# First two tile pairs of each feed-forward stage as plain products, with the sums of x formed beside them

## The chip, the cores and the metric

The kernel runs on one NeuronCore of a Trainium2 chip. The metric is device time in microseconds (us) of one execution, as the median of repeated runs. Times inside an execution come from one profiled execution, counted from the start of its span.

## The reference

One decoder layer for 512 tokens of width 1024, in float32:

```python
x = layer_norm(ALPHA * x + 0.5 * swiglu(x, ffn1_w_gate, ffn1_w_up, ffn1_w_down), ln1_g, ln1_b)
h = x @ w_in                     # q, f, i, g (512 each), conv_val, conv_gate (512 each)
mix = concat(hgrn2(q, f, i, g), conv_module(conv_val, conv_gate)) @ w_out
x = layer_norm(ALPHA * x + mix, ln2_g, ln2_b)
x = layer_norm(ALPHA * x + 0.5 * swiglu(x, ffn2_w_gate, ffn2_w_up, ffn2_w_down), ln3_g, ln3_b)
# swiglu(x) = (silu(x @ w_gate) * (x @ w_up)) @ w_down, hidden width 2816
```

The change lies in the two feed-forward stages (FFN1, FFN2), in their products with `w_gate` and `w_up`.

## The kernel before, in words

**Split operands.** Every float32 operand of a product is split into a high part (a cast on ScalarE, ACT, `cast` L65) and a low part (raw minus high, on VectorE, DVE, `rest` L68; some on POOL). A product of two operands is three matmuls: high x high, high x low, low x high. The splits of one 128x1024 weight tile are kept in a pool `parts` of six slots (`whi`, `wlo`); a slot is written again once TensorE (PE) has read it. The raw weights come through a pool `raws` of two buffers, loaded by SP's queue.

**Tile pairs and seven products.** The hidden width 2816 is 11 pairs of 128-column tiles. For pair `f`, the gate weights (`s` = 0) and the up weights (`s` = 1) are one `Quad` each: four blocks b11, b12, b21, b22, where the first figure is the half of the 1024 inputs and the second the tile of the pair. x is cut likewise into a11, a12, a21, a22 (first figure: half of the tokens, second: half of the inputs); class `Halves` holds these parts. A 2x2 block product is made from seven block products instead of eight (`SEVEN`, `product` L397): p1 = a11 b11, p2 = a12 b21, and five products of sums, as p7 = s3 t3, p5 = s1 t1. The sums of the weights t1 to t4 are formed and split by `Quad.inner`, those of x (s1 to s4) by `Halves.sums`, on DVE. One block product is 4 x 3 = 12 matmuls of 256 columns, so one tile pair (gate and up) is 2 x 7 x 12 = 168 matmuls. `Pair.steps` and `gate_up` combine the products in PSUM into silu(gate) x up.

**The first pair of each stage** is done in two parts: `early` issues p1 and p2 of gate and up (48 matmuls), which need no sums; `ffn` issues the rest (`LATER`), which needs s1 to s4. Pairs 1 to 10 run in the order `USUAL`.

**The start.** SP loads x in four quarters of 512 KB and the first two quads in pieces of 256 and 512 KB, in an order written out by hand (L544 on); then the residual rows `xres` (4 x 512 KB), then the weights of pair 1. POOL's queue loads `vecs` (72 KB). On DVE and ACT the few instructions that form `lb` from `vecs` (L579 to L586) stand ahead of the first splits.

**From one stage to the next.** `rows_out` ends a stage: the last four weight tiles of the down projection are kept, and each of the four token tiles is finished by turns (products, then `add` and `norm` on DVE and POOL). The finished token tile is transposed on PE (`transposed` L259, `transposed_halves` L273), and split into the next operand. PE's order there is written by hand: `follow` gives matmuls of the next stage, of which some are issued ahead of the transposes of the last two token tiles, by the estimates `NORM_WAITS`. At the end of FFN1 it is `four_halved` (the first four products of the mixing stage, in token halves); at the end of the mixing stage, ahead of FFN2, it is `begin`, which gives p1 and p2.

Of the kernel before, what the change touches and what calls it, by code (L numbers as in the profile page):

```python
# [23 lines left out]
NP = NF // 2  # L24
H = T // 2
# [16 lines left out]
BANKS1 = (((0, 2), (1, 3)), ((4, 6), (5, 7))), ((4, 5, 6, 7), (0, 1, 2, 3))  # L42
BANKS2 = (((2, 6), (3, 7)), ((0, 4), (1, 5))), ((0, 1, 4, 5), (2, 3, 6, 7))
# [7 lines left out]
def decoder_layer(ctx, tc, x_tok, x_q, vec, bcast, ng, w_gu1, w_d1, w_i, w_g, w_col, w_o, w_gu2, w_d2, out):  # L51
# [37 lines left out]
    class Quad:  # L89
# [16 lines left out]
        def outer(self, one_by_one=False):  # L106
            if not one_by_one:
                self.both(("b11", "b21"), self.raw[:, 0:4:3, :])
                return
            hi, lo = (t.rearrange("p (a b) -> p a b", a=2) for t in pair_of_parts())  # L110
            self.name(("b11", "b21"), hi, lo)

            def step(i):
                split(self.raw[:, 3 * i, :], hi[:, i, :], lo[:, i, :], nc.vector)
            return step
# [16 lines left out]
    def ahead(n):  # L132

        while todo and sum(r[0] for r in ready) < n:
            what, *args = todo.popleft()
            if what == "unit":
                ready.append([1, fetch(*args)])
            elif what == "quad":
                q = Quad(*args)
                q.load(0, 4)  # L140
                q.outer()
                q.inner()
                ready.append([3, q.of])
            elif what == "two":
                qs = [Quad(a) for a in args]
                for q in qs:
                    q.load(0, 4)
                for q in qs:
                    q.outer()
                    ready.append([1, q.of])  # L150
                todo.extendleft(("inner", q, r) for q, r in reversed(list(zip(qs, list(ready)[-2:]))))
            else:
                q, r = args
                q.inner()
                r[0] += 2
# [4 lines left out]
    def plan_quads(srcs):  # L160
        todo.extend(("quad", s) for s in srcs)

    def plan_two(srcs):
        todo.append(("two", *srcs))
# [9 lines left out]
    plan_quads([w_gu1[f, s] for f in range(1, NP) for s in range(2)])  # L174
# [8 lines left out]
    plan_two([w_gu2[0, s] for s in range(2)])  # L183
    plan_quads([w_gu2[f, s] for f in range(1, NP) for s in range(2)])
# [38 lines left out]
    class Halves:  # L223


        def __init__(self):
            a = [slot(f"xa{i}", (4, 4, H), F32R, f"a{'hl'[i]}") for i in range(2)]
            b = [slot(f"xb{i}", (3, 4, H), F32R, f"b{'hl'[i]}") for i in range(2)]
            self.raw = [slot(t, (2, 4, H), F32, "xr") for t in ("v", "c")]
# [741 lines left out]
```

## Time and profile before

| | us |
|---|---|
| median of 3 runs | 987.46 (987.25 to 988.12) |
| the profiled execution | 987.96 |
| its span | 986.1 |
| PE busy | 934.5 |
| DVE busy | 743.2 |
| ACT busy | 397.8 |

The profiled execution is 0.50 above the median, and 1.86 longer than its span. The page gives for each engine its busy time, and a line of 40 digits, each the busy share of one fortieth of the span (24.65 us) in tenths; PEclk is the granted TensorE clock in the same slices. Matmul records overlap (a matmul's record is longer than the time to the next start), so the rate of PE is read from the starts.

### The profile page before, as it was taken

The numbers are of one execution on the slowest core, as the hardware profiler recorded it, in microseconds if no ns is written. First come the engines' busy times: TensorE is split into PE (matmuls) and PEld (weight loads), VectorE is DVE, ScalarE is ACT, GpSimd is POOL, SyncE is SP. The second block draws the span as 40 slices with busy tenths as digits, with TensorE's granted clock in tenths as the row PEclk, the third lists the DMA queues.
The fourth block names the chain that finished last, engine by engine and source line by source line (L and its number), as shares of the span: only waits on it lengthen the run. The fifth ranks groups of instructions, "written<-read, shape, count | busy, mean of one in ns | idle before, by whom it ended". The sixth has DMA issues, their size and how long they took to land.

```text
span 986.1 us, 14697 instructions
## 1 busy us (share of the span) xinstructions
PE 934.5 (95%) x6096; PEld 855.0 (87%) x6096; DVE 743.2 (75%) x987; ACT 397.8 (40%) x577; POOL 120.4 (12%) x107
## 2 busy tenths in 40 slices
PE   3699999999999999999999999599999999999996
PEld 3599999999888888988888978499999999988885
DVE  5999888887834149799988668988888888762407
ACT  4465555554712113312231632555545555631200
POOL 9000000000000014531252103100000000000002
PEclk9699999999999999999999999799999999999999
DMA  7232323232443322321141050223223231443202
GB/s 258 86 127 91 126 87 128 86 105 89 139 150 86 106 65 86 108 76 53 25 128 40 26 189 1 86 86 112 103 87 128 87 129 65 129 150 102 90 22 85
DMA packets 21202, 96.69 MB, mean 98 GB/s; under 512 B 2368, under 2 KB 2368, under 8 KB 15760
## 3 DMA queue, kind: packets, MB, share of 16 engines
q1 hardware_dynamic: 21024, 95.43, 29.3%
q8 instruction: 47, 0.77, 0.3%
q0 software_dynamic: 112, 0.34, 0.1%
q14 instruction: 19, 0.16, 0.1%
HBM read 93.66 MB, written 2.10 MB: 97 GB/s over the span
## 4 chain that ended last, share of the span: by engine, by line
PE 74%; DVE 15%; issue 4%; POOL 2%; DMA 2%; ACT 2%; POOLq 0%; DVEq 0%; ACTq 0%
PE bank L397 44%; PE bank L190 9%; PE bank L189 9%; PE bank L188 9%; DVE bank L729 4%; PE bank L746 2%; DVE xres L335 2%; DVE wlo L68 1%; POOL wlo L68 1%; DMA raw<-w_col 1%; DMA vecs<-vec 1%; DVE bl L68 1%; DVE m L778 1%; POOL rstd L216 1%; DVE diag L786 1%
## 5 line engine op out<-in xcount | busy, mean ns | idle before, releaser
L68 DVE TENSOR_TENSOR wlo<-raw,whi 128x1024 fp32r<-128x1024 f32 (+1 forms) x144 | 174.0, 1213 | 146.4 <-ACT whi L65 146.2
L65 ACT CAST whi<-raw 128x1024 fp32r<-128x1024 f32 (+1 forms) x166 | 172.3, 1041 | 259.7 <-PE bank L190 140.7
L397 PE MATMUL bank<-bh,whi 128*128 128x256 f32 x528 | 152.0, 288 | 20.3 <-ACT bh L65 18.9
L397 PE MATMUL bank<-ah,whi 128*128 128x256 f32 x528 | 151.6, 287 | 9.8 <-ACT whi L65 9.5
L397 PE MATMUL bank<-bl,whi 128*128 128x256 f32 x528 | 151.9, 288 | 3.5 <-DVE bl L68 3.5
L397 PE MATMUL bank<-al,whi 128*128 128x256 f32 x528 | 151.3, 287 | 1.0 <-DVE al L278 0.8
L397 PE MATMUL bank<-bh,wlo 128*128 128x256 f32 x528 | 151.5, 287 | 0.8 <-DVE wlo L68 0.8
L397 PE MATMUL bank<-ah,wlo 128*128 128x256 f32 x528 | 151.2, 286 | 0.3 <-DVE wlo L68 0.3
L188 PE MATMUL bank<-whi,hp 128*128 128x512 f32 x320 | 124.7, 390 | 0.0
L190 PE MATMUL bank<-whi,hp 128*128 128x512 f32 x320 | 124.5, 389 | 0.0
L189 PE MATMUL bank<-wlo,hp 128*128 128x512 f32 x320 | 124.5, 389 | 0.0
L397 PEld LDWEIGHTS bank<-bh,whi 128*128 128x128 f32 x528 | 103.5, 196 | 21.0 <-ACT bh L65 19.3
L397 PEld LDWEIGHTS bank<-ah,whi 128*128 128x128 f32 x528 | 103.2, 195 | 10.1 <-ACT whi L65 9.5
L397 PEld LDWEIGHTS bank<-bl,whi 128*128 128x128 f32 x528 | 103.5, 196 | 4.1 <-DVE bl L68 4.1
L397 PEld LDWEIGHTS bank<-al,whi 128*128 128x128 f32 x528 | 103.1, 195 | 1.6 <-DVE al L278 1.1
L397 PEld LDWEIGHTS bank<-bh,wlo 128*128 128x128 f32 x528 | 103.5, 196 | 1.1 <-DVE wlo L68 1.1
L397 PEld LDWEIGHTS bank<-ah,wlo 128*128 128x128 f32 x528 | 103.0, 195 | 0.8 <-DVE wlo L68 0.8
L729 DVE SCALAR_TENSOR_TENSOR bank<-u,vecs,bank 128x512 f32<-128x512 f32 x120 | 82.1, 748 | 0.2
L68 DVE TENSOR_TENSOR wlo<-t,whi 128x1024 fp32r<-128x1024 f32 x44 | 54.6, 1242 | 24.9 <-ACT whi L65 24.9
L65 ACT CAST whi<-t 128x1024 fp32r<-128x1024 f32 x44 | 46.1, 1048 | 66.3 <-PE bank L397 62.7
L189 PEld LDWEIGHTS bank<-wlo,hp 128*128 128x128 f32 x320 | 60.1, 188 | 12.5
L188 PEld LDWEIGHTS bank<-whi,hp 128*128 128x128 f32 x320 | 60.1, 188 | 12.4
(184 smaller groups left out, 1772.6 us busy)
## 6 DMA issues: line engine op xcount, KB each, us to landing
raw<-w_gu SPq DMA_DIRECT2D x42, 1024.0 KB, 4.8
raw<-w_d SPq DMA_DIRECT2D x44, 512.0 KB, 3.6
raw<-w_col SPq DMA_DIRECT2D x16, 512.0 KB, 3.5
raw<-w_o SPq DMA_DIRECT2D x8, 512.0 KB, 3.6
xr<-x_q SPq DMA_DIRECT2D x4, 512.0 KB, 7.1
xres<-x_tok SPq DMA_DIRECT2D x4, 512.0 KB, 9.5
gb<-bcast SPq DMA_DIRECT2D x4, 512.0 KB, 4.9
raw<-w_i SPq DMA_DIRECT2D x4, 512.0 KB, 3.5
```

What stands on the lines that cost most here:

```text
L65: nc.scalar.copy(hi, raw)
L68: engine.tensor_tensor(lo, raw, hi.bitcast(F32), op=ALU.subtract)
L188: nc.tensor.matmul(ps, lhsT=lh, rhs=rh, start=first, stop=False)
L189: nc.tensor.matmul(ps, lhsT=lh, rhs=rl, start=False, stop=False)
L190: nc.tensor.matmul(ps, lhsT=ll, rhs=rh, start=False, stop=last)
L216: nc.gpsimd.tensor_tensor(r, r, negh.broadcast_to([P, n]) if n > 1 else negh, op=ALU.pow)
L335: nc.vector.scalar_tensor_tensor(xres[i][:, s], xres[i][:, s], r, bias[:, s], op0=ALU.mult, op1=ALU.add)
L397: nc.tensor.matmul(ps, lhsT=l[:, k, :], rhs=r[:, k, :], start=first and k == 0 and j == 0, stop=k == 3 and j == 2, skip_group_check=True)
L729: nc.vector.scalar_tensor_tensor(accs[n], us[n][:, j:j + T], vecs[:, w:w + 1], accs[n], op0=ALU.mult, op1=ALU.add)
L746: nc.tensor.matmul(ps[:, g, :], lhsT=k[:, h, sl], rhs=q[:, h, sl], start=True, stop=True)
L778: nc.vector.tensor_tensor(ov, ov, tv, op=ALU.mult)
L786: nc.vector.copy_predicated(diag[h], masks[:, n:n + 1, :].broadcast_to([P, NT, P]), ps)
```

## The change

1. Pairs 0 and 1 of each FFN (`PLAIN = 2`) are made as plain products: for each of the two tiles of gate and up, eight blocks of 128 inputs times all 512 tokens, three matmuls each, into one PSUM bank per tile (`plain`: 96 matmuls of 512 columns for a pair). `Halves` therefore keeps a21 too, in the place of s4; s4 is split later, in pair 2, by `last_sum`. `sums` forms the others while the plain pairs run.
2. In FFN1, pair 0's x and weights come in five steps of growing size (one, one, two, two, two of the eight input blocks); each step is one load of x and two of weights, and is split as it comes. PE takes the input blocks in order, over four banks at once.
3. In FFN2, pair 0 is what `begin` now gives: plain too, but in token halves (192 matmuls of 256 columns), the first half ahead of and between the transposes of the last two token tiles.
4. The weights' plan has entries `plain` (2 slots) and `seven` (3 slots) in place of `quad`, `two` and `inner`; banks and slots of both FFNs become the same.

```diff
+        def plain(self):
+            self.both(("b11", "b12"), self.raw[:, 0:2, :])
+            self.both(("b22", "b21"), self.raw[:, 2:4, :])
+        def pieces(self):
...
+            def load(half, a, b):
+                q, sl = slice(2 * half, 2 * half + 2), slice(a * P, b * P)
+                nc.sync.dma_start(out=self.raw[:, q, sl], in_=self.src[:, q, sl])
+            def step(half, a, b):
+                q, sl = slice(2 * half, 2 * half + 2), slice(a * P, b * P)
+                split(self.raw[:, q, sl], hi[half][:, :, sl], lo[half][:, :, sl], nc.vector)
...
+    def plan_quads(src, first):
+        todo.extend(("plain" if f < PLAIN else "seven", src[f, s]) for f in range(first, NP) for s in range(2))
...
+        def rows(self, k, kk=slice(None)):
+            return [t[:, 1:3, kk] if k else t[:, 0:4:3, kk] for t in self.parts]
...
-            self.part("s4", r12)
+        def last_sum(self):
+            self.part("s4", self.quarter(0, 1))
...
+    def plain(banks, x, ws):
+        for ps, (w, l) in zip(banks, ((w, l) for w in ws for l in range(2))):
+            for k in range(NK):
+                xh, xl = x.rows(k // 4, k % 4)
+                mm3(ps, *tile_parts(w, l, k), xh, xl, k == 0, k == NK - 1)
+                yield MM3
+    def begin(begun, x, banks):
+        ahead(4)
+        ws = [unit_now() for _ in range(2)]
+        begun.extend(bank(i, 2, H) for i in banks)
+        for t in range(2):
+            for ps, (w, l) in zip(begun, ((w, l) for w in ws for l in range(2))):
+                for k in range(NK):
+                    xh, xl = x.of[f"a{t + 1}{k // 4 + 1}"]
+                    mm3(ps[:, t], *tile_parts(w, l, k), xh[:, k % 4], xl[:, k % 4], k == 0, k == NK - 1)
+                    yield MM3 / 2
+        ahead(AHEAD)
...
             with tc.manual_schedule(engines={PE}):
-                ahead(3)
-                h.append(h_of(0))
-                for ns in LATER:
...
+                plain_gate_up(begun)
+                for f in range(1, PLAIN):
+                    ahead(4)
+                    ws = [unit_now() for _ in range(2)]
+                    ahead(3)
+                    got = [bank(i, 2, H) for i in chain(*zip(*PAIR_BANKS[f % 2]))]
+                    run(plain(got, x, ws))
+                    plain_gate_up(got)
...
+        for half, a, b in ((0, 0, 1), (0, 1, 2), (0, 2, 4), (1, 0, 2), (1, 2, 4)):
+            raw = x1.raw[half][:, a:b]
+            nc.sync.dma_start(out=raw, in_=x_q[half, :, a:b])
+            for load, _ in pieces:
+                load(half, a, b)
+            xh, xl = x1.rows(half, slice(a, b))
+            split(raw.rearrange("p k t c -> p t k c"), xh, xl, nc.vector)
+            for _, step in pieces:
+                step(half, a, b)
+        begun = [bank(i, 2, H) for i in range(4)]
+        for k in range(NK):
+            xh, xl = x1.rows(k // 4, k % 4)
+            for ps, (w, l) in zip(begun, ((w, l) for w in w0 for l in range(2))):
+                mm3(ps, *tile_parts(w, l, k), xh, xl, k == 0, k == NK - 1)
+        ahead(2)
+        x1.sums()
+        ahead(3)
```

**Three places in the engines' orders.** First, PE in FFN1's pair 0, where the kernel before turns from p2 to p7 (bank0 to bank3 are PSUM banks, `ah`, `al` parts of x, `bh`, `bl` parts of its sums, `whi_N`, `wlo_N` parts of weights). Before:

```order
L397 MATMUL bank1_173<-ah_83,whi_99 128x256
L397 MATMUL bank1_173<-al_84,whi_99 128x256
L397 MATMUL bank1_173<-ah_83,wlo_100 128x256
L397 MATMUL bank2_171<-bh_85,whi_127 128x256
L397 MATMUL bank2_171<-bl_86,whi_127 128x256
L397 MATMUL bank2_171<-bh_85,wlo_128 128x256
```

and at the 49th matmul of the change:

```order
L185 MATMUL bank3_153<-ah_83,whi_101 128x512
L186 MATMUL bank3_153<-al_84,whi_101 128x512
L187 MATMUL bank3_153<-ah_83,wlo_102 128x512
L185 MATMUL bank0_150<-ah_83,whi_99 128x512
L186 MATMUL bank0_150<-al_84,whi_99 128x512
L187 MATMUL bank0_150<-ah_83,wlo_100 128x512
```

Here PE went on with a sum of x (`bh_85`); now it goes on with the second half of the plain weights (`whi_99`), and no sum of x stands in PE's order until pair 2.

Second, DVE at the start of the change (`vecs` is the small load of POOL's queue, `xr` raw x, `raw` raw weights):

```order
L595 TENSOR_TENSOR mx_286<-vecs_79 128x4
L596 TENSOR_TENSOR e_287<-vecs_79,mx_286 128x4
L597 TENSOR_TENSOR e_287<-vecs_79,mx_286 128x4
L69 TENSOR_TENSOR al_84<-xr_87,ah_83 128x2x256
L69 TENSOR_TENSOR wlo_98<-raw_95,whi_97 128x2x128
L69 TENSOR_TENSOR wlo_102<-raw_96,whi_101 128x2x128
L599 TENSOR_TENSOR mx_286<-e_287 128x4
L600 RECIPROCAL mx_286<-mx_286 128x4
L601 TENSOR_TENSOR lb_80<-e_287,mx_286 128x4
L602 TENSOR_SCALAR oml_81<-lb_80 128x4
L69 TENSOR_TENSOR al_84<-xr_87,ah_83 128x2x256
```

All seven small instructions stood ahead of the first split; now three do, and four stand behind the first step. The step is of 512 and twice 256 elements a partition, where it was 1024 and twice 512.

Third, DVE ahead of FFN2, from the split of the second token tile to the norm of the last (`xres3`; `raw_5266` and `raw_5276` are the up weights of pair 0 and the gate weights of pair 1):

```order
L282 TENSOR_TENSOR al_5086<-bank7_5239,ah_5085 128x4x128
L69 TENSOR_TENSOR wlo_5269<-raw_5266,whi_5268 128x1024
L69 TENSOR_TENSOR wlo_5273<-raw_5266,whi_5272 128x1024
L69 TENSOR_TENSOR wlo_5279<-raw_5276,whi_5278 128x1024
L69 TENSOR_TENSOR wlo_5283<-raw_5276,whi_5282 128x1024
L324 SCALAR_TENSOR_TENSOR xres3_76<-bank5_5084,xres3_76 128x512
L282 TENSOR_TENSOR al_5086<-bank6_5316,ah_5085 128x4x128
L325 BN_STATS stats_4948<-xres3_76 128x6
L282 TENSOR_TENSOR al_5086<-bank7_5324,ah_5085 128x4x128
L330 BN_AGGR mv_5288<-stats_4948 128x2
L334 SCALAR_TENSOR_TENSOR xres3_76<-xres3_76,mv_5288,m1_3636 128x512 x2
```

Before, one split of 1024 elements stood ahead of the L321 of `xres3` at this place; now four do.

## Rows read from the trace of the kernel before

**Rows 1.** The page: PE's busy time, and PE, DVE and clock by slices.

```profile
PE 934.5 (95%) x6096; PEld 855.0 (87%) x6096; DVE 743.2 (75%) x987; ACT 397.8 (40%) x577; POOL 120.4 (12%) x107
...
PE   3699999999999999999999999599999999999996
...
PEclk9699999999999999999999999799999999999999
```

**Rows 2.** Stretches: start:end and length, then busy us (instructions) of each engine, PEclk, DMA, GB/s.

```profile
9.49:18.65 9.16, 8.68 (x48) 8.02 (x48) 6.56 (x8) 5.18 (x9) 8.55 (x10) 1.00 1.02 409
18.65:29.60 10.95, 0.14 (x2) 0.00 (x1) 10.95 (x9) 4.18 (x4) 7.76 (x6) 0.66 0.05 18
29.60:42.80 13.20, 9.28 (x38) 8.39 (x38) 13.16 (x14) 5.84 (x8) 0.00 (x0) 0.50 0.23 79
...
52.94:73.48 20.54, 20.52 (x170) 20.26 (x169) 20.41 (x30) 11.53 (x18) 0.00 (x0) 1.00 0.42 143
260.00:360.00 100.00, 100.00 (x442) 82.80 (x442) 38.65 (x37) 25.50 (x25) 0.00 (x0) 1.00 0.36 108
...
626.60:637.26 10.66, 0.84 (x4) 0.30 (x2) 10.66 (x12) 7.36 (x9) 1.78 (x1) 0.65 0.29 98
637.26:643.50 6.24, 6.24 (x29) 6.24 (x30) 6.23 (x6) 1.80 (x3) 0.00 (x0) 0.50 0.01 3
...
388.00:392.00 4.00, 1.98 (x19) 1.77 (x17) 4.00 (x3) 0.59 (x1) 3.17 (x6) 1.00 0.43 132
```

**Rows 3.** The start in order of time: start, us, engine, line, tiles, idle before and releaser.

```profile
7.31 0.16 DVE L579 TENSOR_TENSOR mx<-vecs 128x4 f32<-128x4 f32 x1 [6.39 <-DMA vecs<-vec]
...
8.62 0.74 DVE L586 TENSOR_SCALAR oml<-lb 128x4 f32<-128x4 f32 x1
...
8.95 1.22 DVE L68 TENSOR_TENSOR al<-xr,ah 128x1024 fp32r<-128x1024 f32 x1
...
11.13 0.58 PE L397 MATMUL bank<-ah,wlo 128*128 128x256 f32 x1 [0.33 <-DVE wlo L68]
...
15.14 0.41 PE L397 MATMUL bank<-ah,wlo 128*128 128x256 f32 x1
15.35 0.32 PE L397 MATMUL bank<-ah,whi 128*128 128x256 f32 x1
...
29.60 0.58 PE L397 MATMUL bank<-bh,whi 128*128 128x256 f32 x1 [10.81 <-ACT bh L65]
```

**Rows 4.** DVE in order of time: splits of 512, operations of 256 elements, and one beside POOL.

```profile
21.86 2.05 DVE L241 TENSOR_TENSOR xr<-xr 128x1024 f32<-128x1024 f32 x1
...
38.61 0.68 DVE L68 TENSOR_TENSOR w2lo<-raw,w2hi 128x512 fp32r<-128x512 f32 x1
...
46.47 0.42 DVE L419 TENSOR_TENSOR work<-work 128x256 f32<-128x256 f32 x1
```

**Rows 5.** Loads: line, count, KB each, us from issue to landing (last first-load at 6.39; pair weights).

```profile
raw<-w_gu SPq DMA_DIRECT2D x1, 512.0 KB, 8.9
...
raw<-w_gu SPq DMA_DIRECT2D x42, 1024.0 KB, 4.8
```

**Rows 6.** The norm ahead of FFN2 in order of time, PE and DVE.

```profile
617.37 0.39 PE L397 MATMUL bank<-al,whi 128*128 128x256 f32 x1 [0.81 <-DVE al L278]
...
619.15 1.03 PE L273 MATMUL bank<-ident,xres 128*128 128x128 f32 x8
...
624.68 1.40 DVE L335 SCALAR_TENSOR_TENSOR xres<-xres,rstd,m 128x512 f32<-128x512 f32 x2
...
634.93 0.58 PE L397 MATMUL bank<-bh,whi 128*128 128x256 f32 x1 [8.08 <-ACT bh L65]
637.26 0.58 PE L397 MATMUL bank<-bl,whi 128*128 128x256 f32 x1 [1.75 <-DVE bl L68]
```

**Rows 7.** PE: first matmul of FFN2's third pair; the woven norm ahead of the mixing stage.

```profile
674.72 0.28 PE L397 MATMUL bank<-ah,whi 128*128 128x256 f32 x1
...
391.58 0.63 PE L259 MATMUL bank<-ident,xres 128*128 128x128 f32 x4 [2.02 <-DVE xres L335]
```

More of the change, by code (lines that the diff above doesn't have):

```diff
@@ L24 @@
 NP = NF // 2
+PLAIN = 2
 H = T // 2
@@ L104, in name, with seven @@
                 self.of[n] = tuple(t[:, i, :].rearrange("p (k m) -> p k m", k=4) for t in (hi, lo))
[L106 to L115, printed above, removed]
+        def plain(self):
+            self.both(("b11", "b12"), self.raw[:, 0:2, :])
+            self.both(("b22", "b21"), self.raw[:, 2:4, :])
+        def pieces(self):
+            hi, lo = zip(*(pair_of_parts() for _ in range(2)))
+            hi, lo = ([t.rearrange("p (a b) -> p a b", a=2) for t in ts] for ts in (hi, lo))
+            for names, h, l in zip((("b11", "b12"), ("b22", "b21")), hi, lo):
+                self.name(names, h, l)
+            def load(half, a, b):
[4 more added lines that the diff above has]
+                split(self.raw[:, q, sl], hi[half][:, :, sl], lo[half][:, :, sl], nc.vector)
+            return load, step
+        def seven(self):
+            self.both(("b11", "b21"), self.raw[:, 0:4:3, :])
+            self.inner()
         def inner(self):
@@ L137, in ahead @@
                 ready.append([1, fetch(*args)])
-            elif what == "quad":
+            else:
                 q = Quad(*args)
                 q.load(0, 4)
[L141 to L155, printed above, removed]
+                getattr(q, what)()
+                ready.append([3 if what == "seven" else 2, q.of])
     def plan(srcs, shape, lo_engine):
         todo.extend(("unit", s, shape, lo_engine) for s in srcs)
[L160 to L164, printed above, removed]
+    def plan_quads(src, first):
+        todo.extend(("plain" if f < PLAIN else "seven", src[f, s]) for f in range(first, NP) for s in range(2))
     def unit_now():
@@ L173, in decoder_layer @@
     tok, ch = (2, 512), (NK, P)
-    plan_quads([w_gu1[f, s] for f in range(1, NP) for s in range(2)])
+    plan_quads(w_gu1, 1)
     plan([w_d1[h, u] for h in range(2) for u in range(NP)], tok, nc.vector)
@@ L301, in weave, with rows_out @@
                 owed -= t
-    def rows_out(ks, per, lhs, accs, factor, late, finish, follow=(), before=lambda u: None, then=lambda: None,
-                 fill=True):
+    def rows_out(ks, per, lhs, accs, factor, late, finish, follow=(), before=lambda u: None, then=lambda: None):
         n_units = len(ks) // per
@@ L466, in ffn @@
             h = []
-            w2, pairs = begun
             def gate_up(s, pr):
@@ L494, in ffn @@
                         ahead(3)
-                        pr = Pair(pair_banks[f % 2][s], work_tile() if s else h[f])
-                        run(pr.steps(x, w, USUAL))
+                        pr = Pair(PAIR_BANKS[f % 2][s], work_tile() if s else h[f])
+                        for n in USUAL:
+                            run(pr.steps(x, w, (n,)))
+                            if f == PLAIN and s == 0 and n == "p7":
+                                x.last_sum()
                         gate_up(s, pr)
@@ L532, in lhs @@
                 return tuple(y[:, l * T:(l + 1) * T] for y in hp[f])
-            rows_out(range(NF), 2, lhs, accs, 0.5, 4, finish, follow, before, then)
+            rows_out(range(NF), 2, lhs, FFN_ACCS, 0.5, 4, finish, follow, before, then)
     x1 = Halves()
```

97 lines of the change are left out of this document (33 added, 64 removed).

## The prediction, made before the changed kernel ran

> **What bounds the kernel now.** I read the page first: PE is busy 95% of the span, and its digits are 9 but for slices 1, 2 and 26 and the last [rows 1]; the clock's digits are below 9 in slices 2 and 26 alone. So whole stages run at PE's pace, and time can come back only where PE waits or runs at the lower clock. The stretches say how much that is [rows 2]. From 18.65 to 29.60 PE did next to nothing for 10.95 us, and from 29.60 to 42.80 it was busy 9.28 of 13.20 us at a clock of 0.50 (1.2 GHz, where the full clock is 2.4). The same stands ahead of FFN2: 0.84 busy of 10.66 us from 626.60, then 6.24 us at 0.50. DVE is busy through all of these (10.95 of 10.95, 13.16 of 13.20, 10.66 of 10.66): it forms the sums. The waits name it: PE's first product of a sum waited 10.81 us at 29.60 [rows 3] and 8.08 us at 634.93, then 1.75 us more [rows 6]. In between, PE sets the pace: the second pair took 20.54 us for its 168 matmuls (the row counts 170, with those at its edges) [rows 2], 0.12 each, and a stretch of the down projection did 442 matmuls of 512 columns in 100 us, 0.227 each.
>
> **What the change adds.** A plain pair is 96 matmuls of 512 columns: 96 x 0.227 = 21.8 us, against 168 x 0.12 = 20.2. There are three of these, 3 x 1.6 = 4.9. FFN2's first pair is 192 matmuls of 256 columns: 192 x 0.12 = 23.0, 2.9 more. In all **+7.8 us** of PE work, none of it hidden, since PE is the bound. The operands of the 512-column matmuls lie in two runs of 256, which no row shows; I take 0.227, since a 256-column matmul costs about half of it, so that even two separate passes would be 0.24 (288 matmuls x 0.013 = 3.7 us more).
>
> **What it removes at the start.** Before, pair 2 began at 73.48 [rows 2], that is where two pairs were done. I work out the same point for the change.
>
> DVE still begins with three small instructions that wait for `vecs`, which released it at 7.31 [rows 3]: they end at about 7.8. The first step is then a split of 512 elements, 0.68, and two of 256, 0.42 each [rows 4], against 1.22 [rows 3] and two of 0.68 before: PE's high x low product can start at about 8.5, where it had to wait until 11.13 for the low weights [rows 3]. That `vecs` still lands then is my assumption; if small loads go ahead of it and it comes 2 us later, so does all of this; ACT, with one 8-element instruction behind it, follows.
>
> The steps on DVE: step 1 ends at 9.3; the four small instructions of `lb` behind it are some 1.2 us (the longest took 0.74 [rows 3]; the rest is my estimate), so 10.6; step 2 ends at 12.1; steps 3 to 5 are 1.22 + 2 x 0.68 = 2.6 each and end at 14.7, 17.3, 19.9.
>
> PE starts at the lower clock. Before, it worked closely from 11.13, and the matmuls came closer from 15.4 on [rows 3]: 4.3 us. I take the same 4.3 us from 8.5. At half the clock a 512-column matmul is 0.43 apart (256 columns: 15.14 to 15.35, 0.21 [rows 3]), so PE gets 10 of them done instead of 19, and loses 2.0 us. Its first input block (12 matmuls) ends at about 13.2, and each further block takes 12 x 0.227 = 2.7. So it asks for step 2 at 13.2, for 3 at 15.9, for 4 at 21.4, for 5 at 26.8: all splits are there, by 1.1, 1.2, 4.1 and 6.9 us. Where this cover fails, each us late is a us.
>
> Two pairs then end at 8.5 + 2.0 + 2 x 21.8 = 54.1, if the second pair's weights are in time. Their buffers are free when step 5's gate weights are split (about 19.3); a load of 1 MB lands 4.8 us later [rows 5], at about 24.1. DVE must by then do two sums, a split, a sum and a split (about 1.2 each, or 2.05 beside POOL's scaling of `xres` [rows 4]), and stands at 26 to 28; two splits of the gate weights end at 29 to 31. PE asks for them at 32.3. The cover is 1 to 3 us, the thinnest of this part. The up weights' second half waits for PE's last read of pair 0's gate weights (31.7) and is asked for 11 us later. So pair 2 starts at 54.1 instead of 73.48: **-19.4 us**. From both sides: 8.0 and 3 us of low clock give 53.0 (-20.5); a start at 11.1 as before, 6 us of low clock and 2 us of late splits give 59.5 (-14).
>
> Here **the Trainium skill** speaks against the change. The rows first: the loads of the start ran at 409 GB/s [rows 2], in pieces of 256 and 512 KB; 4.2 MB takes about 10 us, and the last landed at 6.39 + 8.9 = 15.3 [rows 3, 5]. Now the pieces are 128 to 512 KB. "DMA: Bandwidth & Descriptors" (Bandwidth, and Rules for kernel authors) says to batch loads to 1 MiB, and gives 341 GB/s at 1 MB and 138 GB/s at 64 KB; by the latter as an estimate the 4.2 MB would take 30 us. The trace disagrees for loads that follow each other in a queue (409 GB/s at 256 to 512 KB), so I keep the landing near 15.3; what slow loads would do is a rival below.
>
> **What it removes ahead of FFN2.** Before, pair 2 began at 674.72 [rows 7]. Now the first plain product starts where p1 did, waits as long for the low part of the second token tile (617.37 [rows 6], which is 1.1 us after p1's first at 616.28: the wait of 0.81 and a matmul's 0.28), does 192 x 0.12 = 23.0 us, the two transposes in between (0.8 and 1.0 us [rows 6]), and pair 1's 21.8. The wait that can be new is PE's for `xres3`. DVE has four splits ahead of it now, not one: from 617.9 (the half that PE waited for was there at 617.3, the other is 0.6 more), four x 1.15 make 622.5; then the add, two halves of a split and the statistics 0.68 each, the small one 0.2, and four passes of 0.70 (1.40 for two [rows 6]): 628.1, where it was 626.08 [rows 6]. PE arrives after 75 matmuls and a transpose: 617.3 + 9.0 + 0.8 = 627.1. So it waits 1.0 us. Its next need is the split of that transpose, 2.5 us (21 matmuls) later; DVE has a difference, a split of 512 and then that split: just in time. The end: 616.28 + 1.1 + 23.0 + 21.8 + 1.8 + 1.0 = 665.0 against 674.72: **-9.7 us**. The gap is short, and the clock stayed 1.00 in a like one: ahead of the mixing stage the last tile came 2.02 us late [rows 7], with PE busy 1.98 of 4.00 us, and PEclk was 1.00 [rows 2]. From both sides: no wait gives -10.7; a wait of 3 us (2.02 [rows 7], and 1 for passes slowed beside POOL) -7.7.
>
> The sums of weights that DVE and ACT no longer form for eight quads give nothing where PE is the bound. `last_sum` waits for pair 1's last read of a21 and stands on DVE ahead of splits for pair 2's up weights; s4 is used 8 us after pair 2's start, the up weights 10 us after it: hidden, and if not, 1 us.
>
> **The sum.** 987.96 - 19.4 - 9.7 = 958.9 for a profiled execution; both terms hold their part of the 7.8. The median of before was 0.50 below it, so I say **958.5**.
>
> **Rivals.**
> *Late splits or loads at the start.* If the pieces take twice the transfer time (12 us of transfer before the last landed at 15.3, so 27), step 5 is split at about 31, PE does its last two blocks from there, 5.4 us, and pair 0 ends at 36.5: 4 us more, 962.5. If `vecs` is 2 us late, or the clock rises 4 us later, 2 us more each. For it: DVE's cover is 1.1 us at steps 2 and 3, and POOL runs beside it until 20. Against: DVE has nothing else to do, and 409 GB/s. 962 to 966; chance 0.11.
>
> *The clock falls in the norm before FFN2.* The gap with its transposes would have to bring the clock to 0.50 as the 8.08 us wait did [rows 6, 2]. That time it lasted 6.24 us past the wait and cost half of that and more; here I price it as 10 us at half, 5 us: 963 to 965. Against: the row at 388 to 392. Chance 0.07.
>
> *Slower than before.* The two-run operand streams at half rate: each of the 288 matmuls of 512 columns at 0.43, as at the lower clock, instead of 0.227 is +58 us, and 1017 comes out. It decides from 0.227 + 29.1/288 = 0.33 us on. For it: no row shows such an operand. Against: nothing in the 256-column rows hints at a cost per run. Chance 0.02.
>
> *The change does not reach the sums.* PE's order could still put a sum early; the order printed above shows none until pair 2. A stall of DVE's queue that keeps the old length would leave 987 to 995 (the 7.8 alone). Chance 0.01.
>
> **How the numbers follow.** Forecast, 955 to 962: chance 0.79. Late start 0.11, clock 0.07, the other two 0.03. The forecast's own bounds are 987.5 - 20.5 - 10.7 = 956.3 and, with one term at its poor end, 962 to 964. The range takes the forecast whole and most of the two rivals above it: 955 to 964.5. A change under 0.2% (2 us) can't be told from none. All cases but the last two are far below that: faster 0.97, same 0.01, slower 0.02.
>
> **What would show it.** In the changed profile PE's first products lie closely from about 8.5; no wait over 3 us stands in PE's list after that, and none names `bh`; the first 256-column matmul of pair 2 (line of `product`) is at about 54 in FFN1 and about 646 (665.0 - 19.4) in FFN2; plain matmuls of pair 1 stand 0.227 apart; PEclk is 1.00 from about 13 on, and ahead of FFN2. I am wrong about the start if PE waits for `wlo` or `al` between 13 and 33, about the norm if the transposes of the last tile come more than 3 us late or PEclk falls there, and about the added work if the plain matmuls stand more than 0.24 apart.

## The result, and the profile after

The change takes 954.17 us (median of 4 runs, 953.66 to 955.02) where the kernel before took 987.78 on the same chip (4 runs, 987.25 to 988.12): a ratio of 0.9661, 95% interval 0.9644 to 0.9678, so 3.2 to 3.6% faster. Forecast were 958.5 and 955.0 to 964.5. The direction and both mechanisms came true, but the time is 4.3 us under the forecast and 0.8 us under the range. The profiled execution took 953.89 with a span of 952.2, so the spans differ by 33.9 us.

The page of the change, busy time and slices as in [rows 1]:

```profile
PE 932.9 (98%) x5904; PEld 844.3 (89%) x5904; DVE 699.0 (73%) x923; ACT 380.0 (40%) x545; POOL 121.7 (13%) x107
...
PE   7999999999999999999999999999999999999996
...
PEclk9999999999999999999999999999999999999998
```

PE's digits are 9 but in the first and the last slice, and the two dips of the clock are gone. PE's busy time is only 1.6 us less than before (934.5 and 932.9), and its idle time 32.3 us less: in the busy time, less work at half the clock stands against the added work of the plain pairs.

The stretches of the change (start:end and length, then busy us and instructions of PE, PEld, DVE, ACT, POOL, then PEclk, DMA share, GB/s), as in [rows 2]:

```profile
4.12:16.96 12.84, 11.46 (x37) 8.92 (x38) 10.97 (x20) 8.41 (x15) 12.03 (x13) 1.00 1.01 330
11.60:52.18 40.58, 40.58 (x180) 33.59 (x179) 38.12 (x37) 22.26 (x27) 14.87 (x14) 1.00 0.60 219
52.18:72.58 20.40, 20.40 (x170) 20.24 (x169) 16.36 (x22) 11.02 (x16) 0.00 (x0) 1.00 0.28 105
...
602.60:604.00 1.40, 0.17 (x3) 0.05 (x1) 0.96 (x3) 0.61 (x1) 0.45 (x1) 1.00 0.12 47
604.00:641.00 37.00, 36.97 (x221) 32.98 (x222) 27.21 (x29) 17.50 (x22) 1.19 (x1) 1.00 0.17 58
```

From 11.60 to pair 2 PE has no hole. Ahead of FFN2 a hole of 1.23 us is left (in the stretch from 602.60), and the clock stays 1.00 across it. Pair 2 takes 20.40 us, about as the second pair did before (20.54).

The start of the change in order of time, DVE and then PE (start, us, engine, line, operation, tiles, idle before and its releaser), as in [rows 3]:

```profile
4.72 0.64 DVE L595 TENSOR_TENSOR mx<-vecs 128x4 f32<-128x4 f32 x1 [3.80 <-DMA vecs<-vec]
...
5.55 0.68 DVE L69 TENSOR_TENSOR al<-xr,ah 128x512 fp32r<-128x512 f32 x1
6.15 1.37 DVE L69 TENSOR_TENSOR wlo<-raw,whi 128x256 fp32r<-128x256 f32 x2
...
6.29 0.79 PE L186 MATMUL bank<-al,whi 128*128 128x512 f32 x1 [0.38 <-DVE al L69]
6.88 0.63 PE L187 MATMUL bank<-ah,wlo 128*128 128x512 f32 x1
...
11.57 0.41 PE L186 MATMUL bank<-al,whi 128*128 128x512 f32 x1
11.82 0.39 PE L187 MATMUL bank<-ah,wlo 128*128 128x512 f32 x1
...
52.18 0.28 PE L400 MATMUL bank<-ah,whi 128*128 128x256 f32 x1
```

`vecs` released DVE at 4.72, not at 7.31. PE works closely from 6.88, with the matmuls 0.43 apart, and from 11.57 on 0.23 apart. Pair 2 begins at 52.18; it was 73.48.

The norm ahead of FFN2 in the change, DVE and PE, as in [rows 6, 7]:

```profile
592.75 0.39 PE L186 MATMUL bank<-al,whi 128*128 128x256 f32 x1 [0.35 <-DVE al L282]
593.22 5.47 DVE L69 TENSOR_TENSOR wlo<-raw,whi 128x1024 fp32r<-128x1024 f32 x4
598.61 0.68 DVE L324 SCALAR_TENSOR_TENSOR xres<-bank,xres 128x512 f32<-128x512 f32 x1
...
603.98 0.63 PE L279 MATMUL bank<-ident,xres 128*128 128x128 f32 x4 [1.23 <-DVE xres L338]
...
641.03 0.28 PE L400 MATMUL bank<-ah,whi 128*128 128x256 f32 x1
```

The waits of 8.08 and 1.75 us for the sums are gone; 0.35 and 1.23 us for x and for `xres3` are left.

Set end to end, the two traces differ like this:

| stretch | before | change | difference | forecast |
|---|---|---|---|---|
| start to FFN1's pair 2 | 73.48 | 52.18 | -21.3 | -19.4 |
| on to FFN2's first product | to 616.28 | to 592.12 | -2.9 | 0 |
| on to FFN2's pair 2 | to 674.72 | to 641.03 | -9.5 | -9.7 |
| on to the end of the span | to 986.1 | to 952.2 | -0.2 | 0 |

The third row is right. In the first, the forecast is short by 1.9, and the second was not in the forecast at all: the last token tile at FFN1's end, where PE waited 2.02 us before [rows 7], has no wait in the change. Here is that place in the kernel before, POOL and DVE:

```profile
385.57 5.31 POOL L68 TENSOR_TENSOR wlo<-raw,whi 128x1024 fp32r<-128x1024 f32 x2 [0.69 <-ACT whi L65]
...
385.76 5.67 DVE L335 SCALAR_TENSOR_TENSOR xres<-xres,rstd,gb 128x512 f32<-128x512 f32 x2
```

and in the change:

```profile
364.77 5.13 POOL L69 TENSOR_TENSOR wlo<-raw,whi 128x1024 fp32r<-128x1024 f32 x2 [1.79 <-ACT whi L66]
...
363.87 1.41 DVE L338 SCALAR_TENSOR_TENSOR xres<-xres,rstd,gb 128x512 f32<-128x512 f32 x2
...
367.06 1.04 PE L265 MATMUL bank<-ident,xres 128*128 128x128 f32 x8
```

The same two passes over `xres3` take 5.67 us behind POOL's first split of a weight, and 1.41 us ahead of it. The change edits nothing here. My theory after these traces: (a) `vecs` landed early, which gives the 1.9 at the start; (b) a race at FFN1's end gives 2.0 to 2.3 of the middle. A race is here a place where two engines come within tenths of a us of each other and the order decides what follows; I call it lost where POOL's split begins ahead of DVE's two passes, as before, and won where the passes begin first. Most of the rest of the middle is one short wait at 249.91 of the kernel before (0.36) that the change lacks.

### The profile page after: what moved, and what is told of

Read it like the earlier page. It is cut to its first block, busy times and chain, and to the rows that moved or that the text cites. A ratio compares the mean times of both kernels' runs of the same rounds, so it can differ in the third digit from the quotient of the medians.

```text
span 952.2 us, 14214 instructions
## 1 busy us (share of the span) xinstructions
PE 932.9 (98%) x5904; PEld 844.3 (89%) x5904; DVE 699.0 (73%) x923; ACT 380.0 (40%) x545; POOL 121.7 (13%) x107
## 4 chain that ended last, share of the span: by engine, by line
PE 81%; DVE 10%; issue 3%; POOL 2%; DMA 1%; ACT 1%; POOLq 0%; DVEq 0%; ACTq 0%
PE bank L400 38%; PE bank L186 13%; PE bank L187 13%; PE bank L185 13%; DVE bank L745 4%; PE bank L762 2%; POOL wlo L69 1%; DMA raw<-w_col 1%; DVE wlo L69 1%; DVE m L794 1%; POOL rstd L213 1%; DVE fq L712 1%; DVE diag L802 1%; DVE xres L338 0%; DVE totals L798 0%
## 5 line engine op out<-in xcount | busy, mean ns | idle before, releaser
L69 DVE TENSOR_TENSOR wlo<-raw,whi 128x1024 fp32r<-128x1024 f32 (+2 forms) x148 | 176.9, 1201 | 147.8 <-ACT whi L66 147.7
L66 ACT CAST whi<-raw 128x1024 fp32r<-128x1024 f32 (+2 forms) x170 | 173.0, 1022 | 261.0 <-PE bank L187 149.7
L400 PE MATMUL bank<-bh,whi 128*128 128x256 f32 x432 | 122.3, 283 | 0.0
L400 PE MATMUL bank<-bl,whi 128*128 128x256 f32 x432 | 122.3, 283 | 0.0
L400 PE MATMUL bank<-ah,whi 128*128 128x256 f32 x432 | 122.2, 283 | 0.0
L400 PE MATMUL bank<-ah,wlo 128*128 128x256 f32 x432 | 122.2, 283 | 0.0
L400 PE MATMUL bank<-al,whi 128*128 128x256 f32 x432 | 122.2, 283 | 0.0
L400 PE MATMUL bank<-bh,wlo 128*128 128x256 f32 x432 | 122.1, 283 | 0.0
L400 PEld LDWEIGHTS bank<-bh,whi 128*128 128x128 f32 x432 | 82.9, 192 | 0.0
L187 PEld LDWEIGHTS bank<-whi,hp 128*128 128x128 f32 x320 | 60.1, 188 | 12.6
L185 PEld LDWEIGHTS bank<-whi,hp 128*128 128x128 f32 x320 | 60.1, 188 | 12.4
```

Source lines behind the costliest of these rows:

```text
L66: nc.scalar.copy(hi, raw)
L69: engine.tensor_tensor(lo, raw, hi.bitcast(F32), op=ALU.subtract)
L185: nc.tensor.matmul(ps, lhsT=lh, rhs=rh, start=first, stop=False)
L187: nc.tensor.matmul(ps, lhsT=ll, rhs=rh, start=False, stop=last)
L400: nc.tensor.matmul(ps, lhsT=l[:, k, :], rhs=r[:, k, :], start=first and k == 0 and j == 0, stop=k == 3 and j == 2, skip_group_check=True)
```

## Experiments

Each ratio is against runs of the kernel before on the same chip, in four groups: e1, e2, e7, e8 (median of before 988.03); e3 to e6 (986.81); e9, e10, e12 (987.46); e11 (987.47). A difference of about 1 us between times of two groups says nothing.

### The two halves apart

FFN1 as before and FFN2 as in the change, and the other way round:

```diff
+PLAIN1, PLAIN2 = 0, 2
...
+    ffn(x1, begun, load_rest, 0, BANKS1, PLAIN1, after(transposed, 4), four_halved(conv_first, (6, 7, 0, 1)),
...
+    ffn(operand[0], begun, lambda: None, 2, BANKS2, PLAIN2, store)
```

> FFN2 as in the change (plain pairs 0 and 1, pair 0 woven into the norm), FFN1 and the start as before. Theory: the norm's part of the gain stands alone. In the change's trace FFN2's pair 2 came 9.5 us nearer to the first plain product than before (48.9 against 58.4), so about 978.3 against 987.8, and the 2.0 us wait for the last token tile at the end of FFN1 stays, unless the load behind it lands late as in the change's run: then 976. Rival (the two parts share a gain, one needs the other): under 5 us of gain, over 982.5.

Measured: 978.03 (977.38 to 979.76), ratio 0.9901 (0.9881 to 0.9921), 10.0 us under the median of before, 988.03.

> FFN1 and the start as in the change, FFN2 as before. Theory: the start alone is worth 21.3 us (pair 2 at 52.2 instead of 73.5), so about 966.5; with the short wait at FFN1's end gone too (another 2.3 to 2.8 us) 963.7. With e1 the parts add up to the 33.6 of the whole. Rival (the middle's 2.8 us belongs to FFN1's plain pairs themselves): always 963.7, never 966.5.

Measured: 965.26 (963.68 to 967.21), ratio 0.9775 (0.975 to 0.98), 22.8 us under. e1 came out as said; e2's runs lie about both of its values, 963.7 and 966.5. The parts give 10.0 + 22.8 = 32.8, where the whole gave 33.6. In both traces PE waits at FFN1's end as in the kernel before; e1:

```profile
391.54 0.63 PE L301 MATMUL bank<-ident,xres 128*128 128x128 f32 x4 [2.02 <-DVE xres L376]
```

In e2 the wait is 2.01 us, though its start is the change's:

```profile
363.17 5.21 POOL L73 TENSOR_TENSOR wlo<-raw,whi 128x1024 fp32r<-128x1024 f32 x2 [0.80 <-ACT whi L70]
...
363.27 5.66 DVE L376 SCALAR_TENSOR_TENSOR xres<-xres,rstd,gb 128x512 f32<-128x512 f32 x2
```

So the gain in the middle does not follow from either half. Without it the parts should have fallen 2 to 3 us short of the whole; that they did not is no proof against it, since e2's runs spread over 3.5 us. Its profiled run is the fastest, 963.68 with the wait, where 966.5 was expected with it: pair 2 began 0.6 us sooner than in the change (51.61), and FFN2's part up to pair 2 took 57.11 us where the kernel before took 58.44.

### The race at FFN1's end, won and lost on purpose

The kernel before, with POOL held by a small split and two memsets ahead of its first split of a weight (e7):

```diff
-        split(raw, hi, lo, lo_engine)
+        cast(hi, raw)
+        if lo_engine is nc.gpsimd and not late:
+            late.append(1)
+            rest(lo[:, 0:128], raw[:, 0:128], hi[:, 0:128], lo_engine)
+            for _ in range(2):
+                nc.gpsimd.memset(lo.bitcast(F32), 0.0)
+        rest(lo, raw, hi, lo_engine)
```

> The kernel before, with POOL held back by about 2 us (a split of 128 columns and two memsets of 1024) ahead of its first weight split at FFN1's end. Theory: before, DVE's last two passes over xres3 took 2.9 and 2.8 us instead of 0.74 only because POOL's split had started 0.2 us ahead of them; with POOL later they take 0.74 each, PE's wait of 2.02 us for the last tile goes, and the time falls by about 2.3 us to 985.5. Rival (the passes are slow there whatever POOL does, or the wait is another's): 987.8, the wait stays. Other rival: the delayed split is itself late for PE, slower than 988.

Measured: 985.36 (10 runs, 984.27 to 986.32) against 988.03 (13 runs, 986.23 to 989.63), ratio 0.9971 (0.9962 to 0.9981). POOL, DVE and PE of e7:

```profile
388.46 4.75 POOL L68 TENSOR_TENSOR wlo<-raw,whi 128x1024 fp32r<-128x1024 f32 x2
...
386.06 1.62 DVE L343 SCALAR_TENSOR_TENSOR xres<-xres,rstd,gb 128x512 f32<-128x512 f32 x2
...
389.24 1.04 PE L267 MATMUL bank<-ident,xres 128*128 128x128 f32 x8
```

The passes take 1.62 us, PE does not wait, and 2.7 us come back by making POOL later, as forecast (985.5). And the change with DVE's passes put behind (e8):

```diff
+    seen = []
...
+            for c in range(4 if i == NT - 1 and not seen else 0):
+                s = slice(c % 2 * 512, (c % 2 + 1) * 512)
+                nc.vector.tensor_scalar(xres[i][:, s], xres[i][:, s], 1.0, 1.0, op0=ALU.mult, op1=ALU.mult)
+            if i == NT - 1:
+                seen.append(1)
```

> The change, with DVE held back at the same place: four more passes of 512 elements (times 1) over xres3 ahead of the last two, 1.4 to 2.8 us. Theory: POOL's split now starts first, the last two passes take over 2 us each, and PE waits 2 to 5 us for the last tile: 956.5 to 959.5, against 954.2. Rival (the order of POOL and DVE does not matter): the passes stay at 0.74, PE waits at most 1.5 us: below 955.8.

Measured: 959.26 (958.39 to 959.33), ratio 0.9706 (0.9688 to 0.9724), 5.1 us over the change. POOL and DVE, the transposes, and the stretch behind them:

```profile
362.99 5.04 POOL L69 TENSOR_TENSOR wlo<-raw,whi 128x1024 fp32r<-128x1024 f32 x2 [0.71 <-ACT whi L66]
...
363.18 5.81 DVE L339 TENSOR_SCALAR xres<-xres 128x512 f32<-128x512 f32 x4
368.90 1.41 DVE L344 SCALAR_TENSOR_TENSOR xres<-xres,rstd,gb 128x512 f32<-128x512 f32 x2
...
369.79 1.34 PE L266 MATMUL bank<-ident,xres 128*128 128x128 f32 x8 [3.26 <-DVE xres L344]
...
370.90:374.30 3.40, 3.40 (x18) 3.40 (x17) 1.38 (x2) 0.73 (x2) 1.04 (x1) 0.50 0.02 6
```

The wait is 3.26 us, and behind it the granted clock is 0.50 (1.2 GHz) for 3.4 us, which costs half of that: 3.26 + 1.7 = 5.0. The time is as forecast, the passes are not: the last two took 0.74 us each, since they began behind the end of POOL's splits (368.03). It is the four added passes, with one input each, that POOL held: two took 2.63 and 2.58 us beside its splits, the two behind them 0.41 each. At 0.41 the four would take 1.6 us, and in the change PE's transposes came 2.45 us after the end of the first pass (364.61 and 367.06); so the added work would by this estimate have cost PE nothing, had POOL not stood in its way. The place moves the kernel before by 2.7 us, and the change by 5.1 with the added passes.

### How many plain pairs

```diff
-PLAIN = 2
+PLAIN = 1
```

> The change with one plain pair per feed-forward stage instead of two (pair 1 is made of seven products again), nothing else. Theory (two plain pairs are what it takes to hide the sums): PE does 2 x 1.6 = 3.2 us less, but pair 1 asks for its first product of a sum at about 31.5 us, 1.4 us after pair 0's end at 30.3. In the trace of the change DVE ended the growing splits at 19.8 and the first three splits of sums of x at 24.9, 27.2 and 32.3 with two weight splits between; now five passes over pair 1's gate weights (about 5 us) stand among them too, so those sums come between 33 and 38. PE waits 2 to 6 us there, and again less in FFN2; the lower clock may come back. 953 to 960 us in all, with waits of PE on bh or on split weight sums in the trace between 30 and 50 us. Rival (the first plain pair alone gives enough cover): no wait over 1 us there, 954.2 - 3.2 = 951.0.

Measured: 961.95 (961.37 to 962.3), ratio 0.9746 (0.9732 to 0.9761). PE in FFN1's pair 1, and the stretch behind the last of these waits:

```profile
33.05 0.39 PE L400 MATMUL bank<-bl,whi 128*128 128x256 f32 x1 [1.40 <-DVE bl L69]
...
36.00 0.39 PE L400 MATMUL bank<-ah,whi 128*128 128x256 f32 x1 [1.38 <-ACT h L420]
...
44.66 0.58 PE L400 MATMUL bank<-al,w2hi 128*128 128x256 f32 x1 [2.35 <-DVE al L69]
...
44.66:48.07 3.41, 3.41 (x16) 3.41 (x17) 3.41 (x6) 1.51 (x2) 0.00 (x0) 0.50 0.22 55
```

Three waits, 5.1 us in all, and the half clock behind the last. The first is for the low part of a sum of x (`bl`), the second for ACT's `h`, the third for the low part of s4 (`al`, which is split late). So the second plain pair is what hides the sums at the start. In FFN2 PE waited for no sum, with one plain pair there too. Two us over my upper end, since the race was lost here too (2.02 us at 375.66), with 3.41 us at 0.50 behind it (from 375.75). With three pairs:

```diff
-PLAIN = 2
+PLAIN = 3
```

> The change with three plain pairs per feed-forward stage instead of two, nothing else. Theory (PE is the bound and nothing is late in pairs 2 and later): each further plain pair costs its longer time on PE and no more, 96 x 0.227 = 21.8 against 168 x 0.12 = 20.2, so 2 x 1.6 = 3.2 us: 957.4. Rival (the sums of weights that DVE and ACT save are worth something, or s4's late split held pair 2): 954 to 956. Rival on the other side (512-column matmuls on the two-run operand are dearer than 0.227 in the steady state): above 958.5.

Measured: 959.01 (957.85 to 959.66), ratio 0.9716 (0.9701 to 0.9731). On its face that is the rival's "dearer than 0.227". The stages say otherwise: the span is 5.4 us longer, of which 4.3 lie between FFN1's pairs and FFN2 (the race lost again: transposes 2.30 us apart, and the clock at 0.50 from 372.33 for 3.41 us; and a wait of 0.52 at 358.62). The third plain pair costs 96 x 0.227 = 21.8 against 20.4 of a seven-product pair, 1.4 each, 2.8 for two; FFN1's took 21.76. The start and the way through FFN2's first pairs came out 0.5 and 1.2 us shorter (the wait for `xres3` is 0.72 us, not 1.23). 4.3 + 2.8 - 1.7 = 5.4.

### What sets the start

Two steps instead of five:

```diff
-        for half, a, b in ((0, 0, 1), (0, 1, 2), (0, 2, 4), (1, 0, 2), (1, 2, 4)):
+        for half, a, b in ((0, 0, 4), (1, 0, 4)):
```

> The change with pair 0's x and weights of FFN1 loaded and split in two steps of four input blocks each (1 MB of x and two times 512 KB of weights) instead of five growing ones; the same bytes, the same matmuls. Theory (the small first pieces are what brought vecs and the first operands in early): x of the first step lands at about 6.5 to 7, its split on DVE takes about 2.4 us (four times the 512 elements that took 0.68), the low weights follow with 1.2 us each, so PE works closely from about 10 to 11 instead of 6.9; vecs lands at about 7, as in the kernel before. All later steps are covered. Pair 2 starts 3 to 4.5 us later, 957 to 959 in all. Rival (PE's start depends on the small load of vecs alone, which lands early because x is loaded in another order): within 0.5 us of the change, 954.2.

Measured: 960.56 (960.16 to 961.71), ratio 0.9736 (0.9719 to 0.9753): 6.4 us, more than I said. DVE of this kernel:

```profile
8.40 0.16 DVE L595 TENSOR_TENSOR mx<-vecs 128x4 f32<-128x4 f32 x1 [7.48 <-DMA vecs<-vec]
...
11.09 2.29 DVE L69 TENSOR_TENSOR al<-xr,ah 128x2048 fp32r<-128x2048 f32 x1 [0.81 <-ACT ah L66]
```

x had landed at 5.64, but `vecs` (72 KB, issued at 1.36 as in the change) only at 8.37, with 1 MB of x and 512 KB of weights issued ahead of it, and the cast of x stands behind it on ACT. Pair 2 begins at 58.33, 6.1 us late; in part that is `vecs`, in part the larger first splits (2.29 us for x, then 1.31 and 1.43 for the weights). The larger the loads issued ahead of it, the later the small load landed: 4.70 in the change, 7.28 before, 8.37 here. It is not exact: in the seven other runs that load as the change does it landed at 4.61 to 5.70.

Next, `vecs` by itself: POOL is held by two memsets ahead of issuing it, and the orders of DVE and ACT at the start are written out as they were in the change.

```diff
+        with tc.manual_schedule(engines={mybir.EngineType.Pool, mybir.EngineType.DVE, mybir.EngineType.Activation}):
+            for n in range(2):
+                nc.gpsimd.memset(xres[3], 0.0)
+            nc.gpsimd.dma_start(out=vecs, in_=vec)
...
```

> The change with POOL held back by two 1024-element memsets (about 1 us each) ahead of issuing the small load of vecs, and with the order of DVE and ACT kept as it was (the instructions that read vecs stand ahead of the first splits): vecs lands late, about as late as the forecast had assumed (7.3), with everything else early. It measures the disputed assumption by itself. Theory (the forecast was off at the start because vecs landed at 4.70 and not at 7.3): DVE's first instruction waits for vecs although the first x is there at 4.1; PE works closely from 8 to 9 instead of 6.9, pair 2 starts at 53.5 to 55 (the forecast said 54.1 with vecs at 7.3) where three runs with vecs early gave 51.2, 52.2 and 53.3, and the time is 955 to 957. Rival (the start is set by the pieces of x and w, and vecs does not matter): PE works closely from 6.9, 953.2 to 955.

Measured: 956.6 (954.55 to 958.87), ratio 0.9681 (0.9656 to 0.9705). DVE and PE:

```profile
7.02 0.16 DVE L578 TENSOR_TENSOR mx<-vecs 128x4 f32<-128x4 f32 x1 [6.10 <-DMA vecs<-vec]
...
7.37 0.69 DVE L69 TENSOR_TENSOR al<-xr,ah 128x512 fp32r<-128x512 f32 x1
...
9.65 0.63 PE L186 MATMUL bank<-al,whi 128*128 128x512 f32 x1
...
54.07 0.28 PE L400 MATMUL bank<-ah,whi 128*128 128x256 f32 x1
```

With `vecs` at 7.00, nearly where the forecast had assumed it, pair 2 begins at 54.07; the forecast said 54.1. The trace decides here and not the median: the profiled run, at 958.87, lost the race at FFN1's end, and the others (958.03, 955.17, 954.55) lie as if it went either way, which their times alone do not show. The 54.07 is one profile, 0.75 us later than the latest start of pair 2 with `vecs` early (53.32) and 1.9 later than the middle of these (51.0 to 53.3).

Last, `vecs` out of the way altogether, on SP's queue behind the pieces:

```diff
-        nc.gpsimd.dma_start(out=vecs, in_=vec)
+        nc.sync.dma_start(out=vecs, in_=vec)
```

> The change with the small load of vecs issued by SP's queue behind all pieces instead of by POOL's queue, so that the instructions that read it stand behind the splits on DVE and ACT; nothing else. In the trace of the change DVE's first instruction (mx, 4.72) and the two behind it stand ahead of the first split of x, whose operands were there at 4.76 and which began at 5.55. Theory (what is left of the start is this): the first split begins at about 4.8, PE works closely from 0.5 to 0.8 us earlier, pair 2 starts at about 51.5 instead of 52.2, 953.5 in all. Rival (the weights' casts on ACT and their low parts are the last to come): pair 2 starts at 52.2 as before, 954.2. If the time at the lower clock is longer by what PE starts earlier, the gain is half of it.

Measured: 953.78 (953.35 to 954.89), ratio 0.9666 (0.9651 to 0.968), which can't be told from the change. DVE's first split began at 4.70 instead of 5.55, but pair 2 at 52.69 instead of 52.18: the first low weights took 1.03 us, and PE lost 0.4 us behind 30.60, in pair 1. PE worked closely from 6.99, no sooner than in the change. Nothing came of the 0.85 us that DVE began sooner, as the rival said; but the two forecasts are 0.7 us apart, less than the starts of equal kernels spread, so the time does not decide between them.

### A better version

The four splits ahead of `xres3`'s add, cut to two, and POOL held as in e7:

```diff
                 if i == NT - 1:
-                    ahead(SLOTS)
+                    ahead(SLOTS if factor == 0.5 else 4)
```

> The change, with two edits. First, in the norm ahead of FFN2 only two splits of weights stand on DVE ahead of the add into xres3, and one more behind it, where four stood ahead (593.2 to 598.7 in the trace of the change). Second, POOL is held back by about 2 us ahead of its first split of a weight at FFN1's end, so that DVE's last two passes over xres3 always run ahead of it. Theory: the add starts about 2.5 us sooner and a split's 1.2 us stands behind it, so xres3 is finished 1 to 2 us sooner than at 604.5 and PE's gap of 1.5 us ahead of the last transposes of FFN2's side shrinks to under 0.3; at FFN1's end nothing changes, since POOL was already late there. 954.2 - 1.3 = 952.9. Rival (the up weights' splits that now stand behind the add are late for the next products): PE waits there instead, 954 to 956.

Measured: 951.35 (950.93 to 951.73), ratio 0.9629 (0.9613 to 0.9644). The norm ahead of FFN2:

```profile
591.88 2.34 DVE L69 TENSOR_TENSOR wlo<-raw,whi 128x1024 fp32r<-128x1024 f32 x2
594.15 0.67 DVE L332 SCALAR_TENSOR_TENSOR xres<-bank,xres 128x512 f32<-128x512 f32 x1
...
601.25 1.04 PE L287 MATMUL bank<-ident,xres 128*128 128x128 f32 x8
```

No wait stands in front of the transposes. From the third token tile's transposes to pair 2 it is 44.75 us, where the change took 46.50: 1.7 us of the gain lie where the edit is, and the remaining 0.5 to 1 is an earlier start of pair 2 (51.20), where nothing was edited. Then FFN2 with one plain pair, on top:

```diff
-    plan_quads(w_gu2, 0)
+    plan_quads(w_gu2, 0, 1)
...
-    ffn(operand[0], begun, lambda: None, 2, store)
+    ffn(operand[0], begun, lambda: None, 2, store, n_plain=1)
```

> As the one before, with pair 1 of FFN2 made of seven products again, so FFN1 has two plain pairs and FFN2 one. In the run with one plain pair in both, no wait of PE stood in FFN2 behind the last transposes. Theory (there the woven first pair alone hides the sums): 1.6 us of PE's work less, 952.9 - 1.6 = 951.3. Rival (with the add moved forward, the passes over pair 1's weights that stand beside the norm come late): a wait of 1 to 3 us on t4's or t1's low part behind pair 0, 952 to 955.

Measured: 952.33 (5 runs, 950.65 to 953.16), ratio 0.9634 (0.9616 to 0.9651): no gain that can be told. The same stretch is 44.21 us, 0.5 less instead of 1.6; short waits (0.3 to 0.4 us at 592.9, 606.6 and 632.9) take the rest.

> The change itself once more, beside the two above. 953.6 to 955.0 as measured first, if POOL's first split at FFN1's end is late again in every run (the load ahead of it took 4.6 us in the trace, 3.5 in the kernels where PE waited). If that is chance from run to run, runs 2 to 4 us longer are among them.

Measured: 953.58 (953.14 to 954.82), ratio 0.9653 (0.9637 to 0.967). In its profiled run PE does not wait at FFN1's end, as in the first. e9 beats it by 2.2 us, and the runs of the two do not overlap. Between the fastest and the slowest of its runs lie 1.7 us, so none shows the 2 to 4 us of a lost race.

## Why the prediction was right or wrong

Two steps failed. The start took the landing of `vecs` from the kernel before (1.9 us), and the sum had no term for the way from FFN1's pair 2 to FFN2 (2.9 us), where PE's wait of 2.02 us was taken as given. The time missed the range by 0.8 us, so either alone would by the traces have left it inside. The mechanism, holes that the plain pairs fill, was right at both places.

**What bounds the kernel: right.** PE at its pace with holes at two places; the holes closed, PE's share went from 95 to 98%.

**The added work: right, slightly high.** Plain matmuls stand 0.227 apart (median over the 178 starts from 11.60 to 52.18), on two-run operands too, so the half-rate rival fell. A seven-product pair is 20.4 us rather than 20.2, so a plain pair costs 1.4 instead of 1.6.

**The start: the step that failed is "That `vecs` still lands then is my assumption".** -21.3 came instead of -19.4. I took 7.3 us from the kernel before, and the steps from there were good: with `vecs` at 7.00 the same matmuls gave 54.07 for my 54.1. (In part by luck: PE worked closely from 9.65 there, not from 8.5, but had done six products ahead of that; and a single start is not sure to 1 us.) In the change smaller pieces stand ahead of `vecs`, and it landed at 4.70. With PE working closely from 6.88 for 8.5, 4.7 us of lower clock for 4.3 and two products done ahead, my sum gives 52.2, and 52.18 was measured. I had even priced the other side, a later `vecs`, and not this one; as my lower bound of the start I let PE begin 0.5 us sooner.

**The steps behind it: right.** DVE ended step 5 at 19.76 (forecast 19.9), and from 6.88 to pair 2 PE had no wait over 0.25 us. The last first load landed at 16.96, not at 15.3, at 330 GB/s between the first and the last landing where the kernel before moved 409 [rows 2]; that did not matter, since PE asked for it much later. The rival of late loads fell.

**The norm ahead of FFN2: right.** 48.9 us from the first plain product to pair 2 (forecast 48.7), the wait for `xres3` 1.23 us (1.0), and the clock at 1.00.

**The middle: the second step that failed, a term that was missing.** The sum 987.96 - 19.4 - 9.7 puts this stretch at nothing, without a reason. I used the 2.02 us wait at 391.58 [rows 7] as evidence on the clock, and did not ask what made it. It was a race between POOL's split and DVE's passes, decided by 0.2 us, at a place that the change moves in time. In the ten traces where neither engine was held there, the order goes with the wait without exception:

| kernel | POOL's split begins | DVE's two passes begin | they take | PE's fourth and fifth transpose start apart |
|---|---|---|---|---|
| before | 385.57 | 385.76 | 2.90, 2.84 | 2.30 |
| e1 | 385.57 | 385.74 | 2.90, 2.84 | 2.30 |
| e2 | 363.17 | 363.27 | 2.90, 2.84 | 2.28 |
| e3 | 369.71 | 369.85 | 2.90, 2.84 | 2.30 |
| e4 | 365.17 | 365.26 | 2.90, 2.84 | 2.30 |
| e11 | 366.24 | 366.29 | 2.90, 2.84 | 2.29 |
| e12 | 365.97 | 365.65 | 0.75, 2.90 | 0.19 |
| e5 | 370.49 | 370.15 | 0.74, 2.89 | 0.18 |
| e6 | 365.34 | 364.54 | 0.74, 0.74 | 0.11 |
| change | 364.77 | 363.87 | 0.74, 0.74 | 0.11 |

Where only the second pass came behind POOL (e5, e12) PE lost 0.1 us. A pass that begins behind POOL's split ends about 0.55 us after it: in the kernel before POOL's first split ended at 388.11 and the pass at 388.66. The Trainium skill ("SBUF — State Buffer", Who interferes with whom) has the rule: a DVE instruction with two inputs in SBUF contends with a GpSimd instruction that reads SBUF, the ports that they share are an exclusive lock, and the order of issue decides who blocks. The trace agrees: 2.90 us and 0.74 us for the same first pass, when it began 0.05 us behind POOL's split (e11) and 0.32 us ahead of it (e12).

What a lost race costs is 2.0 us of PE's time (3.26 in e8, with its added passes), and in e3, e4, e8 and e11 another 1.7, as the granted clock fell to 0.50 for 3.4 us behind the wait. In before, e1 and e2 it stayed at 1.00 behind the same wait. The change won in both of its profiles (here and e12), but nothing in it puts POOL behind, and e3, e4 and e11, which have the same code at this place, lost: so much of the gain is luck. By an estimate from these prices the change would have taken 956.2 with the race lost, and 957.9 with the lower clock too, inside the range and close to the forecast.

Why POOL was late in the change is settled in part. Its split waits for ACT's cast, and that for the raw weights, which took 4.60 us to land in the change (3.50 before, 4.01 to 4.49 in e5, e6 and e12, 3.52 to 3.64 in e1 to e4 and e11): all six that lost had it in under 3.7, all four that won in over 4.0. What makes the load late stays open. A fetch of instructions (16 KB) lies on the DMA engines beside that load in the change, e6 and e12, but not in e5, and e8 and e11 have one with the load in 3.5 to 3.6 us.

**The sum.** Of the 5.0 us between the forecast for a profiled execution (958.9) and 953.89, 1.9 lie at the start and 2.9 in the middle; the rest is 0.2 against me at the norm, and 0.2 each at the end and outside the span.

## What to carry to other kernels

A landing read from the old trace holds only while the same loads stand ahead of it; when pieces shrink, ask again for every small load behind them. A wait that a change does not touch is still part of the forecast if two engines decide it by a few tenths of a us: look at what starts within a us of it, and price both orders. Where such a race is found, hold the engine that can wait (here POOL: 2.7 us, and PE waited for none of POOL's splits in the trace of e7).

## What the runs showed of the hardware

In the kernels that load and start as the change does, PE's first product came at 5.0 to 5.2 and close work began at 6.9 to 8.4; the matmuls came at the full pace (0.23 instead of 0.43 apart) from about 9.1 us on in e8, 9.4 in e9, 10.5 in e3 and e4, 11.6 in the change, 11.8 in e10 and 12.8 in e12. Pair 2 began at 51.0 to 53.3 with it (51.02, 51.20, 52.18, 52.73 and 53.32 for e8, e9, the change, e10 and e12). So about 2 us of a single profile's start are chance, and the first 1 us of a difference there should not be explained. That holds for the 1.9 us above too: the trace shows `vecs` releasing DVE sooner, but its share in them is not sure to 1 us.

The same wait of 2.0 us was followed by 3.4 us at a clock of 0.50 in three traces (e3, e4, e11) and by none in three others (before, e1, e2): the price of a short wait has two values. The traces differ in what PE did ahead of it. In e3, e4 and e11, and in e8, PE had also waited 0.52 to 0.54 us for `xl`, a low part of x (at 363.21, 358.62, 359.65 and 356.54); in before, e1 and e2 it had not. e12 had that short wait alone, and its clock stayed at 1.00. No run separates the two waits on purpose, so it is not shown that the two together bring the fall.
